# Gate and up products of a macaron decoder layer with the weight tile stationary and the tokens streamed

## The chip, the cores and the metric

One core of a Trainium2 chip runs one program that computes a whole decoder layer. The metric is device time in microseconds: 2391.34 us is the median of three runs (2390.54 to 2392.04). The profile is of one further execution, which took 2391.58 us; its span from the first to the last instruction is 2389.9 us.

## The reference, cut to what matters

```python
def swiglu(h, w_gate, w_up, w_down):
    return (jax.nn.silu(h @ w_gate) * (h @ w_up)) @ w_down

def rmsnorm(x, g):
    y = x * lax.rsqrt(jnp.mean(x * x, axis=-1, keepdims=True) + EPS)
    return y * g

x = x + 0.5 * swiglu(rmsnorm(x, ffn1_norm), ffn1_w_gate, ffn1_w_up, ffn1_w_down)   # half-step 1
h = rmsnorm(x, mix_norm)
mem_n = rmsnorm(mem, mem_norm)
x = x + mixer(h, mem_n, w_in, ..., w_kv_mem, w_branch, w_out)
x = x + 0.5 * swiglu(rmsnorm(x, ffn2_norm), ffn2_w_gate, ffn2_w_up, ffn2_w_down)   # half-step 2
return rmsnorm(x, final_norm)
```

x and mem are 256 tokens of 2048 features, float32. Gate and up weights are 2048 x 5632, the down weights 5632 x 2048. The mixer merges a gated linear attention, a spatial gating and an attention over the memory through 2048 x 12304 input weights, three branch weights of 1024 x 2048 and an output weight of 2048 x 2048.

## The kernel before, in words

All large products run in a rounded float32 format in which TensorE takes one pass per matmul. To keep float32 accuracy every operand is split in two: a rounded high part and the rounded remainder, low. A product is then three matmuls, high by high, high by low, low by high, summed in one PSUM accumulator (`products`, L123 to L125). Activations are kept transposed, as [features, tokens], in a `Split`: tiles of eight feature groups by 256 tokens, high and low. Weights come from HBM in 1 MB tiles `raw` of four feature groups by 512 columns (`load`, L112). `split` makes the parts of half such a tile, two feature groups, in one step: ScalarE casts it to `wh` (L119), VectorE subtracts to get `wl` (L120). `raw`, `wh` and `wl` have three buffers each. A half of a raw tile is called a half step below.

`gemm` runs one column chunk: 512 output features, all 256 tokens as two blocks b of 128, over all feature groups. In every matmul the 128 x 128 piece of the activations is the loaded operand and 512 weight columns stream past it, so the result is [128 tokens, 512 features] in one accumulator for each block.

`ffn` is a half-step of the layer (the reference's swiglu). Its 5632 hidden features are 11 chunks, done as a part of 6 and a part of 5; each part is followed by the four column chunks of the down product over its own features. For each chunk: the gate gemm; Silu with the row's norm factor `rs` (L319, tokens lie on partitions, so the factor is a per-partition scalar); the up gemm; a multiply by factor and Silu result (L323); and `tsplit` for each block, which transposes the four 128 x 128 pieces on TensorE (L166, into a `trp` bank) and splits them into high (L174) and low (L175) of `hT`, the loaded operand of the down product.

PSUM has eight banks, in three pools: four for accumulators `acc`, two for transposes `trp`, two for small products `sml`. The start of the program brings in the memory in four pieces, transposes and scales them (`norm_piece`, L190 and L191) and runs the four chunks of the memory's key and value product. The mixer lies between the half-steps; small generators are advanced one step per half step (`tick`) so that the branches' small work falls between the matmuls of the projections.

No order is written out by hand: the instructions of each engine are put in order ahead of time, by a scheduler that simulates the program with times of its own and hands out free buffers as they come up. So the number of buffers in a pool also sets the order of an engine's list. On the chip each engine then runs its list strictly in that order.

Of the kernel before, what the change touches and what calls it, by code (L numbers as in the profile page):

```python
# [8 lines left out]
F32 = mybir.dt.float32  # L9
# [3 lines left out]
AF = mybir.ActivationFunctionType  # L13
ALU = mybir.AluOpType
AX = mybir.AxisListType
PSUM = bass.MemoryType.PSUM

P = 128
S = 256
NB = S // P  # L20
D = 2048
KT = D // P
DFF = 5632
CW = 512
# [11 lines left out]
class Split:  # L36
# [11 lines left out]
    def l(self, kt, b):  # L48
        return self.lo[kt // 8][:, kt % 8, b * P : (b + 1) * P]

    def four(self, kt, b):
        i, j = kt // 8, kt % 8
        return (
            self.hi[i][:, j : j + 4, b * P : (b + 1) * P],
            self.lo[i][:, j : j + 4, b * P : (b + 1) * P],
        )
# [3 lines left out]
def layer(ctx: ExitStack, tc: tile.TileContext, a: dict, out: bass.AP):  # L60
    nc = tc.nc
    cp = ctx.enter_context(tc.tile_pool(name="cp", bufs=1))
# [1 line left out]
    wp = ctx.enter_context(tc.tile_pool(name="wp", bufs=3))  # L64
    tp = ctx.enter_context(tc.tile_pool(name="tp", bufs=5))
    sp = ctx.enter_context(tc.tile_pool(name="sp", bufs=4))
    pacc = ctx.enter_context(tc.tile_pool(name="pacc", bufs=4, space=PSUM))
    ptr = ctx.enter_context(tc.tile_pool(name="ptr", bufs=2, space=PSUM))
    psm = ctx.enter_context(tc.tile_pool(name="psm", bufs=2, space=PSUM))

    def slot(shape, dtype=F32):
        return big.tile(shape, dtype, name="m8", tag="m8")

    def tmp():
        return tp.tile([P, CW], F32, name="tmp", tag="tmp")

    def acc():
        return pacc.tile([P, CW], F32, name="acc", tag="acc")

    def trp():  # L80
        return ptr.tile([P, CW], F32, name="trp", tag="trp")

    def sml():
        return psm.tile([P, CW], F32, name="sml", tag="sml")

    x0 = a["x"][0]
    mem0 = a["mem"][0]
# [4 lines left out]
    def tick(n=1):  # L92
        for _ in range(n):
            while queue:
                try:
                    next(queue[0])
                    break
                except StopIteration:
                    queue.pop(0)
# [6 lines left out]
    def load(w, row, col, parts=1):  # L106

        raw = wp.tile([P, 4, CW], F32, name="raw", tag="raw")
        n = 4 // parts
        for i in range(0, 4, n):  # L110
            r = row + i * P
            nc.sync.dma_start(  # L112
                raw[:, i : i + n, :],
                w[r : r + n * P, col : col + CW].rearrange("(j p) n -> p j n", p=P),
            )
        return raw
# [7 lines left out]
        nc.tensor.matmul(acc, lhsT=lhs.h(kt, b), rhs=wl, start=False, stop=False)  # L124
        nc.tensor.matmul(acc, lhsT=lhs.l(kt, b), rhs=wh, start=False, stop=last)  # L125

    def gemm(lhs, n_tiles, w, row0, col0, accs, ticks=0, raws=(), tail=0):


        raws = list(raws)  # L130
        held = []
        for g0 in range(0, n_tiles, 4):
            raw = raws.pop(0) if raws else load(w, row0 + g0 * P, col0)
            late = g0 >= n_tiles - 4 * tail
            if late:
                both = [slot([P, 4, CW], F32R) for _ in range(2)]
                held.append((g0, *both))
            for h0 in (0, 2):
                if late:
                    wh, wl = (t[:, h0 : h0 + 2, :] for t in both)  # L140
                else:
                    wh = wp.tile([P, 2, CW], F32R, name="wh", tag="wh")
                    wl = wp.tile([P, 2, CW], F32R, name="wl", tag="wl")
                split(raw[:, h0 : h0 + 2, :], wh, wl)
                if late:
                    continue
                for b in range(NB):
                    for j in range(2):
                        kt = g0 + h0 + j
                        products(  # L150
                            lhs, kt, b, wh[:, j, :], wl[:, j, :], accs[b],
                            kt == 0, kt == n_tiles - 1,
                        )
                tick(ticks)
        for b in range(NB):
            for g0, wh, wl in held:
                for j in range(4):
                    kt = g0 + j
                    products(
                        lhs, kt, b, wh[:, j, :], wl[:, j, :], accs[b], kt == 0, kt == n_tiles - 1  # L160
                    )
# [9 lines left out]
    def tsplit(src, dst, kt, b):  # L171
        ps = transpose4(src).rearrange("p (j t) -> p j t", t=P)
        hi, lo = dst.four(kt, b)
        nc.scalar.copy(hi, ps)  # L174
        nc.vector.tensor_tensor(lo, ps, hi.bitcast(F32), op=ALU.subtract)  # L175
# [34 lines left out]
    def stats(name):  # L210
        return (
            cp.tile([P, NB, NCH], F32, name=f"ss_{name}"),
            cp.tile([P, NB], F32, name=f"rs_{name}"),
        )


    ident = cp.tile([P, P], F32, name="ident")
# [14 lines left out]


    ss_m, rs_m = stats("m")
    mem_s = [slot([P, NB, 2 * CW]) for _ in range(2)]
    memT = Split(slot, KT)
# [4 lines left out]
    first = []  # L241
# [12 lines left out]
    xT = Split(slot, KT)  # L254
# [33 lines left out]
    for c in range(4):  # L288
        accs = [acc() for _ in range(NB)]
# [5 lines left out]
        for b in range(NB):  # L295
            r = rs_m[:, b : b + 1]
            if c < 2:
                t = tmp()
# [8 lines left out]


    def ffn(xT, rs, wg, wu, wd, after, begin=lambda: None, final=False):
        done = 0  # L310
        for part, n_ch in enumerate((6, 5)):
            hT = Split(slot, 4 * n_ch)
            for c in range(n_ch):
                col = (done + c) * CW
                pg = [acc() for _ in range(NB)]
                gemm(xT, KT, wg, 0, col, pg, ticks=1)
                sil = [tmp() for _ in range(NB)]
                for b in range(NB):
                    nc.scalar.activation(sil[b], pg[b], AF.Silu, scale=rs[:, b : b + 1])  # L319
                pu = [acc() for _ in range(NB)]  # L320
                gemm(xT, KT, wu, 0, col, pu, ticks=1)
                for b in range(NB):
                    nc.vector.scalar_tensor_tensor(  # L323
                        out=sil[b], in0=pu[b], scalar=rs[:, b : b + 1], in1=sil[b],
                        op0=ALU.mult, op1=ALU.mult,
                    )
                    tsplit(sil[b], hT, 4 * c, b)
            if part == 1:
                begin()
            for n in range(NCH):  # L330
                pd = [acc() for _ in range(NB)]
                ends = final and part == 1 and n == NCH - 1
                gemm(
                    hT, 4 * n_ch, wd, done * CW, n * CW, pd, ticks=1, tail=2 if ends else 0
                )
                for b in range(NB):
                    xs = x_s[b][:, n * CW : (n + 1) * CW]
                    nc.vector.scalar_tensor_tensor(  # L338
                        out=xs, in0=pd[b], scalar=0.5, in1=xs, op0=ALU.mult, op1=ALU.add
                    )  # L340
                    if part == 1:
                        after(xs, b, n)
            done += n_ch
# [385 lines left out]
    for i in (1, 2, 0):  # L729
        for n in range(NCH):  # L730
            pg = [acc() for _ in range(NB)]
# [89 lines left out]
```

## Time and profile before

| | |
|---|---|
| median of three runs | 2391.34 us |
| profiled execution, span | 2391.58 us, 2389.9 us |
| TensorE matmuls busy | 2372.0 us (99%) |
| weight loads busy | 1961.7 us (82%) |
| VectorE, ScalarE busy | 1270.1 us (53%), 1071.5 us (45%) |
| HBM read | 445.84 MB, 188 GB/s |

Busy times count an engine's own instructions. A matmul's end is modelled and reaches past the start of the next one, so a busy TensorE says that work was queued, not how fast it went; for that one counts starts in a stretch. Matmuls of `acc` are 128 x 512 and those of `trp` 128 x 128; PE stands for TensorE's matmuls, PEld for its weight loads, DVE for VectorE, ACT for ScalarE, SP for the engine that issues the DMAs.

### The profile page before, as it was taken

To read this page: it belongs to the slowest core of one execution; us is meant where nothing else is said; L and a number is where in the kernel's file an instruction comes from. 1 tells how busy PE (TensorE), PEld (TensorE's weight loads), DVE (VectorE), ACT (ScalarE), POOL (GpSimd) and SP (SyncE) were. 2 spreads that over 40 slices of the span, in tenths; PEclk is the share of its full clock that TensorE was granted. 3 is DMA by queue.
4 is the path that set the end of the run, shared out by engine and by line. 5 is a ranking of instruction groups with operands and counts; after the bars stand their busy time and mean duration, and the time that the engine had idled before them with its cause. 6 is when DMAs were issued, how large, how long until landed. Compare 5 with 4: busy or idle time off the path is not lost.

```text
span 2389.9 us, 26431 instructions
## 1 busy us (share of the span) xinstructions
PE 2372.0 (99%) x10746; PEld 1961.7 (82%) x10746; DVE 1270.1 (53%) x1330; ACT 1071.5 (45%) x1265; POOL 59.5 (2%) x57
## 2 busy tenths in 40 slices
PE   8999999999999999999999999999999999999998
PEld 6888888888888888888788888888888888888886
DVE  5644545445445556556765555555454454454454
ACT  6544444344444444435444444445444433444443
POOL 0000000000000001001300000000000000000000
PEclk9999999999999999999999999999999999999999
DMA  7555555555555665454546555655555555555554
GB/s 257 190 188 187 190 194 191 193 193 187 188 194 193 196 210 191 148 169 159 176 159 211 194 194 194 203 185 191 186 189 191 193 189 193 194 184 193 194 191 144
DMA packets 224211, 451.76 MB, mean 189 GB/s; under 512 B 7268, under 2 KB 7336, under 8 KB 223448
## 3 DMA queue, kind: packets, MB, share of 16 engines
q1 hardware_dynamic: 222344, 442.56, 55.8%
q0 software_dynamic: 1744, 7.51, 0.9%
q8 instruction: 84, 1.38, 0.2%
q14 instruction: 39, 0.32, 0.0%
HBM read 445.84 MB, written 4.19 MB: 188 GB/s over the span
## 4 chain that ended last, share of the span: by engine, by line
PE 97%; DVE 1%; issue 1%; ACT 1%; DMA 0%; ACTq 0%; POOLq 0%; POOL 0%; SPq 0%; DVEq 0%
PE acc L124 31%; PE acc L123 31%; PE acc L125 31%; PE trp L166 2%; PE sml L641 0%; DVE wl L120 0%; PE sml L546 0%; PE sml L574 0%; PE sml L449 0%; DMA m<-in_mem_dram 0%; ACT m L658 0%; ACT tmp L180 0%; ACT wh L119 0%; PE sml L695 0%; PE sml L508 0%
## 5 line engine op out<-in xcount | busy, mean ns | idle before, releaser
L120 DVE TENSOR_TENSOR wl<-raw,wh 128x1024 fp32r<-128x1024 f32 x828 | 1029.4, 1244 | 1025.4 <-ACT wh L119 1024.8
L119 ACT CAST wh<-raw 128x1024 fp32r<-128x1024 f32 x828 | 871.5, 1053 | 1162.4 <-PE acc L125 1143.0
L124 PE MATMUL acc<-wl,m 128*128 128x512 f32 x3312 | 1294.7, 391 | 1.8 <-DVE wl L120 1.7
L125 PE MATMUL acc<-wh,m 128*128 128x512 f32 x3312 | 1290.6, 390 | 0.1
L123 PE MATMUL acc<-wh,m 128*128 128x512 f32 x3312 | 1184.2, 392 | 1.8 <-ACT wh L119 0.9
L124 PEld LDWEIGHTS acc<-wl,m 128*128 128x128 f32 x3312 | 622.6, 188 | 132.2 <-DVE wl L120 3.2
L123 PEld LDWEIGHTS acc<-wh,m 128*128 128x128 f32 x3312 | 622.2, 188 | 131.7 <-ACT m L190 2.2
L125 PEld LDWEIGHTS acc<-wh,m 128*128 128x128 f32 x3312 | 622.1, 188 | 127.5 <-DVE m L191 0.5
L190 ACT ACTIVATE m<-trp,gT 128x128 fp32r<-128x128 f32 x128 | 43.0, 364 | 23.7 <-PE trp L166 14.3
L174 ACT CAST m<-trp 128x512 fp32r<-128x512 f32 x64 | 34.9, 588 | 40.9 <-PE trp L166 40.9
L175 DVE TENSOR_TENSOR m<-trp,m 128x512 fp32r<-128x512 f32 x64 | 41.8, 687 | 21.2 <-ACT m L174 20.9
L191 DVE SCALAR_TENSOR_TENSOR m<-trp,gT,m 128x128 fp32r<-128x128 f32 x128 | 41.3, 347 | 13.4 <-ACT m L190 12.2
L166 PEld LDWEIGHTS trp<-ident,tmp 128*128 128x128 f32 x288 | 34.6, 140 | 6.7
L166 PE MATMUL trp<-ident,tmp 128*128 128x128 f32 x288 | 40.0, 272 | 0.0
L319 ACT ACTIVATE tmp<-acc,rs 128x512 f32<-128x512 f32 x44 | 30.1, 690 | 19.5 <-PE acc L125 19.5
L180 ACT ACTIVATE tmp<-m 128x512 f32<-128x512 f32 x40 | 24.8, 623 | 15.4 <-DVE m L338 11.8
L323 DVE SCALAR_TENSOR_TENSOR tmp<-acc,rs,tmp 128x512 f32<-128x512 f32 x44 | 30.9, 744 | 0.0
L338 DVE SCALAR_TENSOR_TENSOR m<-acc,m 128x512 f32<-128x512 f32 x32 | 20.9, 684 | 9.7 <-PE acc L125 9.4
L203 POOL TENSOR_TENSOR rs<-rs,mhalf 128x1 f32<-128x1 f32 x8 | 4.3, 552 | 868.5 <-DVE rs L200 868.5
L166 PE MATMUL trp<-ident,m 128*128 128x128 f32 x160 | 22.8, 280 | 2.8 <-DMA m<-in_mem_dram 2.8
L166 PEld LDWEIGHTS trp<-ident,m 128*128 128x128 f32 x160 | 19.6, 144 | 6.6 <-DMA m<-in_mem_dram 2.9
L661 POOL TENSOR_TENSOR m<-m,m 128x1024 f32<-128x1024 f32 x7 | 20.9, 2991 | 115.3 <-ACT m L658 87.8
(136 smaller groups left out, 389.1 us busy)
## 6 DMA issues: line engine op xcount, KB each, us to landing
raw<-in_w_in_dram SPq DMA_DIRECT2D x96, 1024.0 KB, 5.0
raw<-in_ffn_w_gate_dram SPq DMA_DIRECT2D x88, 1024.0 KB, 5.1
raw<-in_ffn_w_up_dram SPq DMA_DIRECT2D x88, 1024.0 KB, 5.1
raw<-in_ffn_w_down_dram SPq DMA_DIRECT2D x88, 1024.0 KB, 5.1
raw<-in_w_branch_dram SPq DMA_DIRECT2D x24, 1024.0 KB, 5.1
raw<-in_w_out_dram SPq DMA_DIRECT2D x16, 1024.0 KB, 5.1
raw<-in_w_kv_mem_dram SPq DMA_DIRECT2D x14, 1024.0 KB, 5.1
m<-in_mem_dram SPq DMA_DIRECT2D x4, 512.0 KB, 8.3
```

The costliest lines, as they stand in the source:

```text
L119: nc.scalar.copy(wh, raw)
L120: nc.vector.tensor_tensor(wl, raw, wh.bitcast(F32), op=ALU.subtract)
L123: nc.tensor.matmul(acc, lhsT=lhs.h(kt, b), rhs=wh, start=first, stop=False)
L124: nc.tensor.matmul(acc, lhsT=lhs.h(kt, b), rhs=wl, start=False, stop=False)
L125: nc.tensor.matmul(acc, lhsT=lhs.l(kt, b), rhs=wh, start=False, stop=last)
L166: nc.tensor.transpose(out=ps[:, j * P : (j + 1) * P], in_=src[:, j * P : (j + 1) * P], identity=ident)
L174: nc.scalar.copy(hi, ps)
L175: nc.vector.tensor_tensor(lo, ps, hi.bitcast(F32), op=ALU.subtract)
L190: nc.scalar.activation(dst.h(kt, b), pj, AF.Copy, scale=g)
L191: nc.vector.scalar_tensor_tensor(out=dst.l(kt, b), in0=pj, scalar=g, in1=dst.h(kt, b).bitcast(F32), op0=ALU.mult, op1=ALU.subtract,)
L319: nc.scalar.activation(sil[b], pg[b], AF.Silu, scale=rs[:, b : b + 1])
L323: nc.vector.scalar_tensor_tensor(out=sil[b], in0=pu[b], scalar=rs[:, b : b + 1], in1=sil[b], op0=ALU.mult, op1=ALU.mult,)
```

## The change

In the gate and up gemms the 128 x 128 piece of the weights becomes the loaded operand, and the activations' 256 tokens stream past it (`turned_products`). The result is [128 features, 256 tokens], four accumulators `acct` for a chunk of 512 features, each half a bank of data in a bank of its own. The result is already laid out as the down product needs it, so `tsplit` is not called there any more; `hT` is filled by a copy and a subtraction from SBUF. Tokens now lie along the free dimension, so the norm factor can no longer be a per-partition scalar: `token_factor` transposes it once per half-step into a row that all partitions hold, and VectorE multiplies by that row, before Silu (from PSUM) and after it. The three PSUM pools become one of eight banks for all uses. The down product and the mixer's gemms keep their form.

```diff
-    pacc = ctx.enter_context(tc.tile_pool(name="pacc", bufs=4, space=PSUM))
-    ptr = ctx.enter_context(tc.tile_pool(name="ptr", bufs=2, space=PSUM))
-    psm = ctx.enter_context(tc.tile_pool(name="psm", bufs=2, space=PSUM))
+    ps8 = ctx.enter_context(tc.tile_pool(name="ps8", bufs=8, space=PSUM))
...
+    def acct():
+        return ps8.tile([P, S], F32, name="acct", tag="ps")
...
+    def turned_products(rhs, kt0, wh, wl, accs, first, last):
+        for f in range(4):
+            fs = slice(f * P, (f + 1) * P)
+            for j in range(2):
+                hi, lo = rhs.both(kt0 + j)
+                w = wh[:, j, fs]
+                nc.tensor.matmul(accs[f], lhsT=w, rhs=hi, start=first and j == 0, stop=False)
+                nc.tensor.matmul(accs[f], lhsT=w, rhs=lo, start=False, stop=False)
+                nc.tensor.matmul(
+                    accs[f], lhsT=wl[:, j, fs], rhs=hi, start=False, stop=last and j == 1
+                )
...
+    def token_factor(rs, name):
+        ps = trp()
+        for b in range(NB):
+            nc.tensor.transpose(
+                out=ps[:, b * P : (b + 1) * P], in_=rs[:, b : b + 1].to_broadcast([P, P]),
+                identity=ident,
+            )
+        row = cp.tile([P, S], F32, name=name)
+        nc.vector.tensor_copy(row, ps[:, :S])
+        return row
...
-                pg = [acc() for _ in range(NB)]
-                gemm(xT, KT, wg, 0, col, pg, ticks=1)
-                sil = [tmp() for _ in range(NB)]
-                for b in range(NB):
-                    nc.scalar.activation(sil[b], pg[b], AF.Silu, scale=rs[:, b : b + 1])
-                pu = [acc() for _ in range(NB)]
-                gemm(xT, KT, wu, 0, col, pu, ticks=1)
-                for b in range(NB):
-                    nc.vector.scalar_tensor_tensor(
-                        out=sil[b], in0=pu[b], scalar=rs[:, b : b + 1], in1=sil[b],
-                        op0=ALU.mult, op1=ALU.mult,
-                    )
-                    tsplit(sil[b], hT, 4 * c, b)
+                pg = [acct() for _ in range(4)]
+                gemm(xT, KT, wg, 0, col, pg, ticks=1, turned=True)
+                if row is None:
+                    row = token_factor(rs, f"row{final:d}")
+                sil = [tmp() for _ in range(2)]
+                for i in range(2):
+                    for f in range(2):
+                        nc.vector.tensor_tensor(
+                            sil[i][:, f * S : (f + 1) * S], pg[2 * i + f], row, op=ALU.mult
+                        )
+                    nc.scalar.activation(sil[i], sil[i], AF.Silu)
+                    nc.vector.tensor_tensor(pairs(sil[i]), pairs(sil[i]), along(row), op=ALU.mult)
+                pu = [acct() for _ in range(4)]
+                gemm(xT, KT, wu, 0, col, pu, ticks=1, turned=True)
+                for i in range(2):
+                    for f in range(2):
+                        h = sil[i][:, f * S : (f + 1) * S]
+                        nc.vector.tensor_tensor(h, pu[2 * i + f], h, op=ALU.mult)
+                    hi, lo = hT.two(4 * c + 2 * i)
+                    nc.scalar.copy(hi, pairs(sil[i]))
+                    nc.vector.tensor_tensor(lo, pairs(sil[i]), hi.bitcast(F32), op=ALU.subtract)
```

TensorE's list at the program's first instructions, before (`gm` are the memory's norm gains, `m8_89` and `m8_90` the first and second half of the memory's features, `m8_91` and `m8_93` the high and low parts of its transposed form):

```order
L230 MATMUL trp_97<-ident_79,gm_95 128x16
L166 MATMUL trp_101<-ident_79,m8_89 128x128 x4
L166 MATMUL trp_114<-ident_79,m8_89 128x128 x4
L123 MATMUL acc_227<-wh_229,m8_91 128x512
L123 MATMUL acc_228<-wh_229,m8_91 128x512
L124 MATMUL acc_227<-wl_230,m8_91 128x512
L125 MATMUL acc_227<-wh_229,m8_93 128x512
```

And the same place of the changed kernel (`m8_83` and `m8_84` are the two halves of the memory, `m8_85` the high part):

```order
L275 MATMUL trp_91<-ident_73,gm_89 128x16
L193 MATMUL trp_95<-ident_73,m8_83 128x128 x4
L193 MATMUL trp_108<-ident_73,m8_83 128x128 x4
L193 MATMUL trp_125<-ident_73,m8_83 128x128 x4
L193 MATMUL trp_138<-ident_73,m8_83 128x128 x4
L193 MATMUL trp_155<-ident_73,m8_84 128x128 x4
L193 MATMUL trp_168<-ident_73,m8_84 128x128 x4
L193 MATMUL trp_184<-ident_73,m8_84 128x128 x4
L193 MATMUL trp_197<-ident_73,m8_84 128x128 x4
L131 MATMUL acc_221<-wh_223,m8_85 128x512
L132 MATMUL acc_221<-wl_224,m8_85 128x512
```

Before, eight transposes of the first memory piece stand ahead of the first product, and the other 24 further down, between products. In the changed list all 32 stand ahead of it, those of the second half too.

TensorE's list in half-step 1 at the end of one chunk's up product and the start of the next chunk's gate product, before (`acc_1623` and `acc_1624` are the next gate's accumulators, `tmp_1465` and `tmp_1466` the finished chunk):

```order
L124 MATMUL acc_1624<-wl_1644,m8_220 128x512
L125 MATMUL acc_1624<-wh_1643,m8_222 128x512
L166 MATMUL trp_1608<-ident_79,tmp_1465 128x128 x4
L166 MATMUL trp_1616<-ident_79,tmp_1466 128x128 x4
L123 MATMUL acc_1624<-wh_1643,m8_220 128x512
L124 MATMUL acc_1624<-wl_1644,m8_220 128x512
L125 MATMUL acc_1624<-wh_1643,m8_222 128x512
```

The same engine at such a place of the changed kernel (`acct_2993` belongs to the up product that ends, `acct_3236` and `acct_3237` to the next gate product; `m8_214` to `m8_217` hold the activations):

```order
L144 MATMUL acct_2993<-m8_217,wh_3198 128x256
L145 MATMUL acct_2993<-m8_215,wl_3199 128x256
L143 MATMUL acct_3236<-m8_214,wh_3242 128x256
L144 MATMUL acct_3236<-m8_216,wh_3242 128x256
L145 MATMUL acct_3236<-m8_214,wl_3243 128x256
L143 MATMUL acct_3236<-m8_214,wh_3242 128x256
L144 MATMUL acct_3236<-m8_216,wh_3242 128x256
L145 MATMUL acct_3236<-m8_214,wl_3243 128x256
L143 MATMUL acct_3237<-m8_214,wh_3242 128x256
L144 MATMUL acct_3237<-m8_216,wh_3242 128x256
```

The eight transposes are gone, one product follows on the other; each matmul writes 256 columns and there are twice as many.

VectorE's list over one chunk of half-step 1, before (the gate product ends within the first row, the up product before the second):

```order
L120 TENSOR_TENSOR wl<-raw,wh 128x1024 x14
L323 SCALAR_TENSOR_TENSOR tmp<-acc,rs_219,tmp 128x512 x2
L120 TENSOR_TENSOR wl<-raw,wh 128x1024 x2
L175 TENSOR_TENSOR m_988<-trp,m_985 128x4x128 x2
L120 TENSOR_TENSOR wl<-raw,wh 128x1024 x14
```

And of the changed kernel (`row_1262` is the token row, L367 and L371 the multiplies by it before and after Silu, L377 the multiply of up by the Silu result, L380 the low part of `hT`):

```order
L367 TENSOR_TENSOR tmp<-acct,row_1262 128x256
L128 TENSOR_TENSOR wl<-raw,wh 128x1024
L367 TENSOR_TENSOR tmp<-acct,row_1262 128x256 x3
L128 TENSOR_TENSOR wl<-raw,wh 128x1024
L371 TENSOR_TENSOR tmp<-tmp,row_1262 128x512 x2
L128 TENSOR_TENSOR wl<-raw,wh 128x1024 x6
L377 TENSOR_TENSOR tmp<-acct,tmp 128x256
L128 TENSOR_TENSOR wl<-raw,wh 128x1024
L377 TENSOR_TENSOR tmp<-acct,tmp 128x256 x3
L128 TENSOR_TENSOR wl<-raw,wh 128x1024
L380 TENSOR_TENSOR m_984<-tmp,m_981 128x512 x2
```

At the end of the gate product, where VectorE had nothing but splits, six multiplies now stand among three splits; at the end of the up product four multiplies and two subtractions take the place of two multiplies and two subtractions.

## Rows read from the trace of the kernel before

**Rows 1.** The page: busy time of each engine; the chain's shares by engine.

```profile
PE 2372.0 (99%) x10746; PEld 1961.7 (82%) x10746; DVE 1270.1 (53%) x1330; ACT 1071.5 (45%) x1265; POOL 59.5 (2%) x57
...
PE 97%; DVE 1%; issue 1%; ACT 1%; DMA 0%; ACTq 0%; POOLq 0%; POOL 0%; SPq 0%; DVEq 0%
```

**Rows 2.** Windows: down products; one chunk. Columns: busy (instructions) by engine, clock, DMA, GB/s.

```profile
420.00:520.00 100.00, 100.00 (x443) 82.80 (x442) 48.50 (x43) 39.04 (x37) 0.00 (x0) 1.00 0.59 192
...
689.36:733.77 44.41, 44.41 (x203) 36.86 (x202) 22.21 (x20) 19.22 (x21) 0.00 (x0) 1.00 0.57 189
```

**Rows 3.** Timeline of TensorE around a chunk's transposes: start us, us, engine, line.

```profile
732.98 1.03 PE L166 MATMUL trp<-ident,tmp 128*128 128x128 f32 x8
733.77 0.48 PE L123 MATMUL acc<-wh,m 128*128 128x512 f32 x1
734.09 0.40 PE L124 MATMUL acc<-wl,m 128*128 128x512 f32 x1
```

**Rows 4.** Timeline of VectorE and ScalarE in a gate product, idle time before in brackets.

```profile
713.18 1.22 DVE L120 TENSOR_TENSOR wl<-raw,wh 128x1024 fp32r<-128x1024 f32 x1 [1.49 <-ACT wh L119]
...
714.82 1.05 ACT L119 CAST wh<-raw 128x1024 fp32r<-128x1024 f32 x1 [1.67 <-PE acc L125]
```

**Rows 5.** Timeline of TensorE: low-rank projection (L449) between wide products; the following load.

```profile
768.54 0.28 PE L449 MATMUL sml<-m,gh 128*16 128x256 f32 x1
768.65 0.28 PE L449 MATMUL sml<-m,gl 128*16 128x256 f32 x1
768.77 0.39 PE L449 MATMUL sml<-m,gh 128*16 128x256 f32 x2
769.00 0.39 PE L124 MATMUL acc<-wl,m 128*128 128x512 f32 x1
769.23 0.39 PE L125 MATMUL acc<-wh,m 128*128 128x512 f32 x1
769.46 0.40 PE L123 MATMUL acc<-wh,m 128*128 128x512 f32 x1
...
768.89 0.19 PEld L124 LDWEIGHTS acc<-wl,m 128*128 128x128 f32 x1
```

**Rows 6.** Timeline of TensorE: scores of the linear attention (L641).

```profile
1126.66 1.27 PE L641 MATMUL sml<-m 128*128 128x128 f32 x10
1127.69 0.48 PE L124 MATMUL acc<-wl,m 128*128 128x512 f32 x1
```

**Rows 7.** Groups by line and form: count, busy us, mean ns, idle before.

```profile
L641 PEld LDWEIGHTS sml<-m 128*128 128x128 f32 x128 | 18.1, 190 | 2.0
...
L323 DVE SCALAR_TENSOR_TENSOR tmp<-acc,rs,tmp 128x512 f32<-128x512 f32 x44 | 30.9, 744 | 0.0
...
L175 DVE TENSOR_TENSOR m<-trp,m 128x512 fp32r<-128x512 f32 x64 | 41.8, 687 | 21.2 <-ACT m L174 20.9
...
L748 DVE TENSOR_TENSOR m<-m,tmp 128x512 f32<-128x512 f32 x16 | 10.3, 685 | 0.0
...
L512 DVE SCALAR_TENSOR_TENSOR tmp<-sml,gT,m 128x256 f32<-128x256 f32 x8 | 3.9, 483 | 3.3 <-PE sml L508 3.3
```

**Rows 8.** Timeline of the start, SyncE and TensorE.

```profile
7.07 0.38 SPq L244 DMA_DIRECT2D m<-in_mem_dram  x1
...
5.65 1.97 PE L166 MATMUL trp<-ident,m 128*128 128x128 f32 x8 [2.82 <-DMA m<-in_mem_dram]
8.20 1.22 PE L123 MATMUL acc<-wh,m 128*128 128x512 f32 x2 [0.58 <-ACT wh L119]
...
12.62 0.63 PE L123 MATMUL acc<-wh,m 128*128 128x512 f32 x1
13.04 0.63 PE L124 MATMUL acc<-wl,m 128*128 128x512 f32 x1
```

**Rows 9.** DMA issues from 7 to 8.6 us: count, size, median us to landing.

```profile
m<-in_mem_dram SPq DMA_DIRECT2D x2, 512.0 KB, 9.5
```

**Rows 10.** Window of the start, TensorE's matmuls into `acc` alone.

```profile
8.00:41.40 33.40, 30.73 (x109) 1.00 0.80 294
```

More of the change, by code (lines that the diff above doesn't have):

```diff
@@ L49, in l, with both, two @@
         return self.lo[kt // 8][:, kt % 8, b * P : (b + 1) * P]
+    def both(self, kt):
+        return self.hi[kt // 8][:, kt % 8, :], self.lo[kt // 8][:, kt % 8, :]
+    def two(self, kt):
+        i, j = kt // 8, kt % 8
+        return self.hi[i][:, j : j + 2, :], self.lo[i][:, j : j + 2, :]
     def four(self, kt, b):
@@ L77, in acc @@
     def acc():
-        return pacc.tile([P, CW], F32, name="acc", tag="acc")
+        return ps8.tile([P, CW], F32, name="acc", tag="ps")
+    def acct():
+        return ps8.tile([P, S], F32, name="acct", tag="ps")
     def trp():
-        return ptr.tile([P, CW], F32, name="trp", tag="trp")
+        return ps8.tile([P, CW], F32, name="trp", tag="ps")
     def sml():
-        return psm.tile([P, CW], F32, name="sml", tag="sml")
+        return ps8.tile([P, CW], F32, name="sml", tag="ps")
     x0 = a["x"][0]
@@ L125, in products, with gemm @@
         nc.tensor.matmul(acc, lhsT=lhs.l(kt, b), rhs=wh, start=False, stop=last)
-    def gemm(lhs, n_tiles, w, row0, col0, accs, ticks=0, raws=(), tail=0):
+    def turned_products(rhs, kt0, wh, wl, accs, first, last):
[9 more added lines that the diff above has]
+                )
+    def gemm(lhs, n_tiles, w, row0, col0, accs, ticks=0, raws=(), tail=0, turned=False):
         raws = list(raws)
@@ L145, in gemm @@
                 if late:
+                    continue
+                if turned:
+                    kt = g0 + h0
+                    turned_products(lhs, kt, wh, wl, accs, kt == 0, kt == n_tiles - 2)
+                    tick(ticks)
                     continue
@@ L214, in stats, with pairs, along @@
         )
+    def token_factor(rs, name):
[8 more added lines that the diff above has]
+        return row
+    def pairs(ap):
+        return ap.rearrange("p (f t) -> p f t", t=S)
+    def along(row):
+        return row.unsqueeze(1).to_broadcast([P, 2, S])
     ident = cp.tile([P, P], F32, name="ident")
@@ L309, in ffn @@
     def ffn(xT, rs, wg, wu, wd, after, begin=lambda: None, final=False):
-        done = 0
+        done, row = 0, None
         for part, n_ch in enumerate((6, 5)):
```

## The prediction

> **What bounds the kernel now.** I read the page's busy line first, then the chain that ended last, then windows of single stretches, then the timeline of the places that the change touches. TensorE is busy for 99% of the span and the chain lies on it for 97% [rows 1]. A busy share alone could hide waits, so the pace counts: in the hundred microseconds from 420 to 520, which hold down products only, 443 matmuls touch the window. Two are cut by its edges, so about 441 fit, or 226.7 ns for one 512-column matmul with its own 128x128 weight load, at the upper clock level of 2.4 GHz (granted clock 1.00) [rows 2]. The time of this kernel is therefore the length of TensorE's list, and a change is worth what it does to that list.
>
> One column chunk of 512 features in a half-step takes 44.41 us [rows 2]. Its gate and up products are 2 x 16 x 2 x 3 = 192 matmuls: 192 x 226.67 ns = 43.52 us. The other 0.89 us is the eight transposes that turn the chunk's result: they start at 732.98, the next product starts at 733.77, and the one behind it only 314 ns later instead of 227 [rows 3]. Nothing else in the chunk stops TensorE. VectorE and ScalarE follow it: of each half step of 2.72 us (12 matmuls, one split of 1024 weight columns) ScalarE waits 1.67 us for TensorE and VectorE 1.49 us for ScalarE [rows 4].
>
> **The change, part by part.**
>
> *Transposes that go.* 22 chunks (11 in each half-step) lose eight each: 22 x 0.89 = 19.7 us off the path. Nothing takes their place on TensorE except four transposes in all for the token row: about 0.5 us at the 0.11 us of rows 3.
>
> *Matmuls that change shape.* 22 x 192 = 4224 matmuls of 512 columns become 8448 of 256 columns. The multiplied work is the same; the weight loads double. If 256 columns take half of 512, 113.3 ns, this costs nothing; every nanosecond above that costs 8.4 us. So this one number decides the sign. The trace has 256-column matmuls in the same number format, those of the low-rank projection: four that start at 768.54 end with the next product's start at 769.00, 115 ns each [rows 5]. The last of them had the 128x128 load of the following product beside it (issued at 768.89), so a full load goes under 256 columns in about 113 ns. Against that stands that the 512-column products behind the four start 230 and 230 ns apart (rounded as the rows have it), a little slower than the settled 226.7, and that these are short bursts with 16-column loads between them. The other near row is the score products of the linear attention: ten pairs of a 128x128 load and a 128-column two-pass matmul run from 1126.66 to 1127.69 [rows 6], 103 ns each with both ends counted. Loads at that rate would fit under 113. Bounds: 0 from the proportional reading; below it I see no reason, since the 512-column pace is already the proportional one; above it 6.7 ns, if the 13.3 ns by which 226.7 exceeds 512/2.4 = 213.3 is paid by every matmul whatever its width (106.7 + 13.3 = 120.0; 56 us in all). I take 0, since 115 for the burst is nearer to 113.3 than to 120.
>
> The Trainium skill ("Perfetto Trace Analysis", section Identifying the Most-Contended Engine) says the reverse of the busy line: TensorE's headroom is to be judged by the weight loads' busy share. Here that share is 82% already [rows 1], and 4224 more loads of 188 ns would take it past the span. The 128 score loads last 190 ns each, 24.3 us in sum, and cover only 18.1 us [rows 7]: loads overlap each other, so the sum of their lengths is no bound. By the rule the change would cost hundreds of microseconds, by the row nothing; it is kept as a rival below.
>
> *Work that moves to VectorE and ScalarE.* A chunk gains on VectorE eight 256-column multiplies (0.48 each by the nearest row that reads the accumulators) and four 512-column ones (0.69), 6.6 us, and loses two of 0.74 and two of 0.69, 2.9 us [rows 7]; with 22.2 us busy in 44.4 [rows 2] it goes to about 26. ScalarE keeps two Silu and two copies. The cover is the three-deep split buffers: a split ends 2.3 us after its buffers come free and is needed after 5.4 [rows 4]. The order puts one multiply, a split, three multiplies, a split, and the last two multiplies behind the gate product. The split queued in the middle waits on ScalarE for two Silu (1.4 us), which wait for the last multiplies, 0.5 us behind the product's end: 0.5 + 1.4 + 1.05 + 1.23 = 4.2 us of the 5.4. The stall is zero, with a margin of a microsecond at each of the 44 product ends; if it ran out by 0.2 us each it would cost 9 us.
>
> *PSUM in one pool.* Gate and up take four banks each, all eight, but the gate's come free within 2 us of its end and are needed 21 us later. The mixer shares the eight too. Before, no wait for a bank stands among TensorE's; I take 0, bounds -2 (more room) and +5.
>
> *The start.* This is the part the diff does not show. With two transpose banks only eight transposes of the memory went ahead of the first product, the others lay between products. With eight banks all 32 go first, in TensorE's own order, and they need the last memory piece. Its last two pieces are issued from 7.07 on, one behind the other [rows 8], and land a median 9.5 us after issue [rows 9]; I take 18 us for the later one. Eight cold transposes took 1.97 us [rows 8]. So the first product starts at 18 + 2 = about 20 us instead of 8.20. Then TensorE is cold: before, the matmuls after 12.62 start 420 ns apart (two decimals), which is 512/1.2 = 427 ns at the lower clock level, 1.2 GHz [rows 8], and some thirteen products had passed when they quickened. I allow as many again: 13 x 427 ns end at 25.6, then one per 226.7 ns makes 70 more by 41.4, 83 in all. Before, 109 matmul records lie between 8.00 and 41.40 [rows 10]. The deficit is 26 x 0.2267 = 5.9 us. Bounds: 3 us, if the many early transposes already raise the clock; 8 us, if the splits behind the 16 norm pieces come late as well.
>
> **Sum.** -19.7 + 0.5 + 0 + 0 + 0 + 5.9 = -13.3 us. The profiled execution took 2391.6 us, of which 2389.9 are the span; the median of the runs shown is 2391.3, the same within 0.02%. So 2378 us.
>
> **Rivals.**
>
> *The narrow products never settle at half.* Mechanism: a 256-column matmul in a long run keeps the 117 ns that the middle ones of the burst show (768.65 to 768.77 and on to 769.00, two starts merged) [rows 5], because a load is in flight nearly all the time. 8448 x 3.7 = +31 us: 2409, slower than before. For it: the burst's mean is 115 and the wide products behind it are slow too. Against it: part of the burst is at 113, and the score pairs ran faster. It turns the result into a loss from 13.3 / 8.448 = 1.6 ns on, that is 114.9 ns per matmul. At 120 ns (the fixed-excess bound) it would be 2434.
>
> *Half way.* The pace is 114 to 115.5, and the start and the excess eat the transposes' gain: 2387 to 2396, no change that can be told.
>
> *Loads bind.* Each load holds the path for its 188 ns: 8448 x (188 - 113.3) = +631 us, about 3010. The overlap in rows 7 speaks against it.
>
> The page named above would give this last time. A further page, "TensorE: Matmul & The Clock Gate" of the Trainium skill (section LDWEIGHTS), puts a load at its columns over 1.2 GHz, an estimate of 107 ns for 128 columns: by that it just hides under 113 ns, and no run here shows it for a long run.
>
> *The start is cheaper or dearer, all else as forecast:* 2375 to 2381; it moves the number, not the sign.
>
> **How the numbers follow.** What a measurement of this kernel can tell from no change is 0.2%, 4.8 us. Forecast with its neighbours (2370 to 2386): 0.53. Half way: 0.13. Narrow products at 117 to 120: 0.30. Loads bind or worse: 0.04. That the change does nothing at all is excluded by TensorE's order, where the transposes are gone. Faster 0.53, same 0.13, slower 0.34. Both signs hold weight, so the range reaches from 2371 (start at its low bound, mixer a little better) to 2414 (117 ns plus some of the mixer's bound); the likeliest case's own range is 2371 to 2384.
>
> **What would show it.** In the changed trace: a chunk of 43.5 us with 384 matmuls starting 113.3 ns apart says that the pace is half; 45 says 117. No transposes inside the half-steps' chunks. The first 512-column product at about 20 us, not 8. ScalarE's and VectorE's splits still ending their waits on TensorE and not the reverse; TensorE waiting for a split at a product's end would prove the cover too thin. The prediction is wrong if the pace passes 114.9 ns, or if TensorE waits for accumulators.

## The result and the profile after

The changed kernel takes 2448.49 us (median of 4 runs, 2447.72 to 2448.66), the kernel before on the same chip 2391.28 us: ratio 1.0238, 95% interval 1.0226 to 1.0251. It is 57.2 us slower; 13 us faster was forecast, and the range ended at 2414.

The page of the changed kernel: the engines, to be held against [rows 1], and one of its new groups (count, busy us, mean ns, idle before):

```profile
PE 2412.2 (99%) x14798; PEld 2167.2 (89%) x14798; DVE 1324.3 (54%) x1508; ACT 1064.2 (43%) x1266; POOL 60.7 (2%) x57
...
L145 PE MATMUL acct<-m,wl 128*128 128x256 f32 x2816 | 795.9, 283 | 0.0
```

TensorE is still 99% busy, and the new group (L143 and L144 have as many and read the same) shows no idle time. From the busy line alone nothing looks lost. The pace tells. Windows of the changed kernel, gate and up products first, then down products:

```profile
150.00:250.00 100.00, 100.00 (x836) 100.00 (x835) 52.32 (x59) 40.85 (x43) 0.00 (x0) 1.00 0.56 181
...
420.00:520.00 100.00, 100.00 (x443) 82.84 (x442) 48.87 (x43) 38.86 (x37) 0.00 (x0) 1.00 0.59 192
```

The down products have the 443 matmuls of [rows 2]. In the gate and up products 836 touch the window; less some two and a half that its edges cut, 833.5 fit, so one starts every 120.0 ns at granted clock 1.00. A matmul is shown as 283 ns long and a load as 192, so both rows are full at 100.00 at any pace from 192 down; only the count separates 113 from 120.

The same from VectorE's side (its timeline, with idle time before in brackets; L377 multiplies the up's accumulators, L128 are the splits; a gate product ended at 183):

```profile
160.04 0.42 DVE L377 TENSOR_TENSOR tmp<-acct,tmp 128x256 f32<-128x256 f32 x1 [1.42 <-PE acct L145]
...
189.13 1.23 DVE L128 TENSOR_TENSOR wl<-raw,wh 128x1024 fp32r<-128x1024 f32 x1 [0.51 <-ACT wh L127]
192.00 1.23 DVE L128 TENSOR_TENSOR wl<-raw,wh 128x1024 fp32r<-128x1024 f32 x1 [1.64 <-ACT wh L127]
...
206.12 0.42 DVE L377 TENSOR_TENSOR tmp<-acct,tmp 128x256 f32<-128x256 f32 x1 [1.42 <-PE acct L145]
```

From one up product's end to the next, 160.04 to 206.12, a chunk takes 46.08 us, where [rows 2] have 44.41 with the transposes in it: 384 x 120.0 ns and no stop. The splits start 2.87 us apart, 24 matmuls, and wait for ScalarE; even the one behind the six multiplies and two Silu of the gate's end (189.13) was held 0.51 us by ScalarE and not by VectorE's own work.

The waits of TensorE (line, what it waited for, us in all, times, longest) are new, however; before had 2.8 us for the memory [rows 8], 2.5 for the identity matrix and 3.4 for splits and norm pieces, and nothing else:

```profile
PE trp L193 <- DMA m<-in_mem_dram: 10.1, 3, 4.9
PE trp L193 <- DVE m L801: 5.9, 4, 1.5
...
PE trp L193 <- ACT tmp L581: 1.9, 2, 1.6
PE acc L132 <- DVE wl L128: 1.2, 1, 1.2
PE trp L193 <- DVE m L391: 1.1, 4, 0.3
PE trp L193 <- DVE m L815: 1.1, 4, 0.3
PE trp L193 <- ACT tmp L344: 0.4, 1, 0.4
```

Only one is for a split. The others are transposes (L193) of results that VectorE or ScalarE has just made, outside the chunks. The worst of them on TensorE's timeline, in the mixer:

```profile
1488.10 0.39 PE L133 MATMUL acc<-wh,m 128*128 128x512 f32 x1
1489.98 1.26 PE L193 MATMUL trp<-ident,m 128*128 128x128 f32 x8 [1.48 <-DVE m L801]
1490.99 0.47 PE L131 MATMUL acc<-wh,m 128*128 128x512 f32 x1
```

The transposes stand directly behind the last matmul of the product whose result they turn. TensorE starts nothing for 1.88 us where 0.23 is usual: 1.65 us lost, 1.48 of them shown as idle. Before, work of the next product stood between (L748 is the line that L801 has become):

```profile
1462.34 0.69 DVE L748 TENSOR_TENSOR m<-m,tmp 128x512 f32<-128x512 f32 x1
...
1466.28 0.62 PE L123 MATMUL acc<-wh,m 128*128 128x512 f32 x2
1466.73 1.03 PE L166 MATMUL trp<-ident,m 128*128 128x128 f32 x8
```

VectorE was done at 1463.03, 3.7 us before the transposes began, and TensorE had matmuls until then.

The start, to be held against [rows 8]:

```profile
10.09 1.97 PE L193 MATMUL trp<-ident,m 128*128 128x128 f32 x8 [2.46 <-DMA m<-in_mem_dram]
16.92 3.67 PE L193 MATMUL trp<-ident,m 128*128 128x128 f32 x16 [4.86 <-DMA m<-in_mem_dram]
20.25 0.78 PE L131 MATMUL acc<-wh,m 128*128 128x512 f32 x1
20.82 0.63 PE L132 MATMUL acc<-wl,m 128*128 128x512 f32 x1
...
22.53 0.51 PE L133 MATMUL acc<-wh,m 128*128 128x512 f32 x1
22.88 0.40 PE L131 MATMUL acc<-wh,m 128*128 128x512 f32 x1
```

The first product starts at 20.25 us, as foreseen: by the trace the last memory piece landed at 18.26. The lower clock level of the first matmuls is read from their spacing, here as in [rows 8] (20.82 to 22.53 are four steps of 427 ns, 512 columns at 1.2 GHz); the clock column of the windows reads 1.00 for this stretch in both kernels, [rows 10] too.

### The profile page after: what moved, and what is told of

It reads as the page before. It is cut to its first block, busy times and chain, and to the rows that moved or that the text cites. A ratio compares the mean times of both kernels' runs of the same rounds, so it can differ in the third digit from the quotient of the medians.

```text
span 2446.9 us, 34812 instructions
## 1 busy us (share of the span) xinstructions
PE 2412.2 (99%) x14798; PEld 2167.2 (89%) x14798; DVE 1324.3 (54%) x1508; ACT 1064.2 (43%) x1266; POOL 60.7 (2%) x57
## 3 DMA queue, kind: packets, MB, share of 16 engines
q8 instruction: 115, 1.88, 0.3%
## 4 chain that ended last, share of the span: by engine, by line
PE 96%; DVE 2%; ACT 1%; issue 1%; DMA 1%; SPq 0%; ACTq 0%; POOLq 0%; POOL 0%; DVEq 0%
PE acc L132 17%; PE acc L133 17%; PE acc L131 17%; PE acct L144 14%; PE acct L145 14%; PE acct L143 14%; PE trp L193 1%; DVE wl L128 1%; ACT wh L127 1%; PE sml L694 1%; DMA m<-in_mem_dram 0%; PE sml L599 0%; PE sml L627 0%; PE sml L502 0%; DMA raw<-in_w_kv_mem_dram 0%
## 5 line engine op out<-in xcount | busy, mean ns | idle before, releaser
L128 DVE TENSOR_TENSOR wl<-raw,wh 128x1024 fp32r<-128x1024 f32 x828 | 1027.1, 1241 | 978.7 <-ACT wh L127 978.5
L143 PE MATMUL acct<-m,wh 128*128 128x256 f32 x2816 | 797.0, 283 | 0.0
L144 PE MATMUL acct<-m,wh 128*128 128x256 f32 x2816 | 796.7, 283 | 0.0
L145 PE MATMUL acct<-m,wl 128*128 128x256 f32 x2816 | 795.9, 283 | 0.0
L132 PE MATMUL acc<-wl,m 128*128 128x512 f32 x1904 | 743.8, 391 | 1.3 <-DVE wl L128 1.2
L133 PE MATMUL acc<-wh,m 128*128 128x512 f32 x1904 | 742.7, 390 | 0.0
L131 PE MATMUL acc<-wh,m 128*128 128x512 f32 x1904 | 688.4, 393 | 0.0
L144 PEld LDWEIGHTS acct<-m,wh 128*128 128x128 f32 x2816 | 540.6, 192 | 0.1
L143 PEld LDWEIGHTS acct<-m,wh 128*128 128x128 f32 x2816 | 540.6, 192 | 0.1
L145 PEld LDWEIGHTS acct<-m,wl 128*128 128x128 f32 x2816 | 540.2, 192 | 0.0
L132 PEld LDWEIGHTS acc<-wl,m 128*128 128x128 f32 x1904 | 357.9, 188 | 75.4 <-DVE wl L128 2.4
L133 PEld LDWEIGHTS acc<-wh,m 128*128 128x128 f32 x1904 | 357.8, 188 | 74.1
L131 PEld LDWEIGHTS acc<-wh,m 128*128 128x128 f32 x1904 | 357.7, 188 | 73.3 <-issue 0.8
L377 DVE TENSOR_TENSOR tmp<-acct,tmp 128x256 f32<-128x256 f32 x88 | 33.8, 422 | 31.1 <-PE acct L145 31.1
L367 DVE TENSOR_TENSOR tmp<-acct,row 128x256 f32<-128x256 f32 x88 | 33.5, 421 | 28.4 <-PE acct L145 28.4
L193 PE MATMUL trp<-ident,m 128*128 128x128 f32 x160 | 27.5, 311 | 18.4 <-DMA m<-in_mem_dram 10.1
L193 PEld LDWEIGHTS trp<-ident,m 128*128 128x128 f32 x160 | 20.4, 157 | 27.5 <-DMA m<-in_mem_dram 11.0
L371 DVE TENSOR_TENSOR tmp<-tmp,row 128x512 f32<-128x512 f32 x44 | 28.3, 685 | 0.2 <-ACT tmp L370 0.2
```

Source lines behind the costliest of these rows:

```text
L128: nc.vector.tensor_tensor(wl, raw, wh.bitcast(F32), op=ALU.subtract)
L131: nc.tensor.matmul(acc, lhsT=lhs.h(kt, b), rhs=wh, start=first, stop=False)
L143: nc.tensor.matmul(accs[f], lhsT=w, rhs=hi, start=first and j == 0, stop=False)
L144: nc.tensor.matmul(accs[f], lhsT=w, rhs=lo, start=False, stop=False)
L145: nc.tensor.matmul(accs[f], lhsT=wl[:, j, fs], rhs=hi, start=False, stop=last and j == 1)
L193: nc.tensor.transpose(out=ps[:, j * P : (j + 1) * P], in_=src[:, j * P : (j + 1) * P], identity=ident)
```

## The experiments

Theory: a matmul with a 128-column load in this number format takes its columns at 2.4 GHz and 13.3 ns more, whatever its width, so cutting 512 into two of 256 adds 6.7 ns per narrow matmul. Rivals: the turned form itself is slow (weights loaded right after they are written, tokens streamed); the evacuation work starves TensorE; the single pool does it. Differences below are taken from 2391.28 us; the kernel before, run again beside the experiments, had medians of 2390.74 and, for the last two, 2391.23 us, and the ratios are to these, so half a microsecond of a difference means nothing.

**Narrow matmuls in the old form.** The kernel before, with its three pools, its orientation and its transposes; only the gate and up matmuls are cut in two, except the first of each accumulator.

```diff
-                        products(
+                        (narrow_products if narrow else products)(
...
+        for i in range(2):
+            cs = slice(i * S, (i + 1) * S)
+            for k, (x, w) in enumerate(pairs):
+                nc.tensor.matmul(
+                    acc[:, cs], lhsT=x, rhs=w[:, cs], start=False,
+                    stop=last and i == 1 and k == len(pairs) - 1,
+                )
```

> The kernel before with one thing changed: in the gate and up gemms every 512-column matmul is cut into two of 256 columns, with the same loaded activations, the same accumulators, transposes and pools (the first matmul of each accumulator stays whole). Of the 192 matmuls of a chunk 188 become 376. Theory 1, every matmul pays about 13.3 ns on top of its columns (256 columns: 120.0 ns): 22 x (376 x 0.120 - 188 x 0.22667) = +55 us, 2446 us, and a chunk of 46.9 us. Rival, the pace of 120 ns comes from the turned form (weights as the loaded operand, just written by ScalarE and VectorE): 2391 us, a chunk stays at 44.4 us.

Measured 2446.14 us, ratio 1.0231 (1.0216 to 1.0247): +54.9 us. Its window of gate and up products:

```profile
150.00:250.00 100.00, 100.00 (x829) 99.60 (x829) 48.05 (x44) 40.56 (x43) 0.00 (x0) 1.00 0.55 180
```

Cut are 4224 - 88 matmuls, into 8272: x 6.67 ns = 55.2 us. The count of 829 is that of 120.0 ns with the chunks' transposes and a few whole matmuls in the window; from one up product's multiplies to the next (154.75 to 201.64 in its trace) a chunk takes 46.89 us, the 46.9 of theory 1. Halving the width, which doubles the loads with it, costs the whole amount with neither the turned form nor its evacuation nor the one pool. The rivals on form and evacuation are not needed.

**The change with the pools of before.** Gate accumulators in the four banks of `acc`, the up's in the two of `trp` and the two of `sml`.

```diff
-    def acct():
-        return ps8.tile([P, S], F32, name="acct", tag="ps")
+    def acct(i, up):
+        pool, tag = (pacc, "acc") if not up else (ptr, "trp") if i < 2 else (psm, "sml")
+        return pool.tile([P, S], F32, name="acct", tag=tag)
```

> The changed kernel with the three PSUM pools of before (4 + 2 + 2 banks; gate accumulators in the four, up accumulators in the other four). Theory, the single pool costs the 15 to 20 us beyond the narrow matmuls, by the order it gives TensorE's list at the start and in the mixer: first product at about 8 us, no wait of 1.9 us ahead of the transposes of the mixer, total 2391.3 - 19.7 + 56.3 + 0.5 = 2428 us. Rival, these microseconds come from the turned products themselves (other engines late, other transfers): about 2448 us as the changed kernel.

Measured 2428.87 us, ratio 1.0159 (1.0144 to 1.0174). Waits of TensorE and the window:

```profile
PE trp L196 <- DMA m<-in_mem_dram: 2.9, 1, 2.9
...
PE acc L135 <- DVE wl L131: 1.8, 3, 0.9
```

```profile
150.00:250.00 100.00, 100.00 (x836) 100.00 (x835) 54.79 (x64) 41.34 (x45) 0.00 (x0) 1.00 0.56 185
```

The pace is the same 836, the waits are those of the kernel before, and the first product starts at 8.33 us. So the turned products with their transposes saved cost 2428.87 - 2391.28 = 37.6 us, which is 56.3 - 19.7 + 0.5 = 37.1 by the terms; the pool costs the other 2448.49 - 2428.87 = 19.6 us.

**One pool, and nothing else.** The kernel before with its three pools made one of eight banks.

```diff
-    pacc = ctx.enter_context(tc.tile_pool(name="pacc", bufs=4, space=PSUM))
-    ptr = ctx.enter_context(tc.tile_pool(name="ptr", bufs=2, space=PSUM))
-    psm = ctx.enter_context(tc.tile_pool(name="psm", bufs=2, space=PSUM))
+    ps8 = ctx.enter_context(tc.tile_pool(name="ps8", bufs=8, space=PSUM))
```

> The kernel before with one thing changed: one PSUM pool of eight banks for all. Theory, as for the kernel with three pools: the start costs 5.4 us and the mixer 11.8 us as in the changed kernel, and the transposes of each chunk, which now stand directly behind the up product in TensorE's list, wait about 0.5 us each for VectorE: 22 x 0.5 = 11 us more; 2391.3 + 5.4 + 11.8 + 11 = 2420 us. Rival, the pool is innocent: 2391 us.

Measured 2427.48 us, ratio 1.0154 (1.0137 to 1.0171): +36.2 us, more than expected. Waits of TensorE, then its timeline at the end of a chunk in half-step 1:

```profile
PE trp L164 <- DMA m<-in_mem_dram: 10.1, 3, 4.9
PE trp L164 <- DVE tmp L321: 7.6, 22, 0.3
PE trp L164 <- DVE m L746: 5.9, 4, 1.5
```

```profile
158.03 0.39 PE L123 MATMUL acc<-wh,m 128*128 128x512 f32 x1
158.77 1.31 PE L164 MATMUL trp<-ident,tmp 128*128 128x128 f32 x8 [0.35 <-DVE tmp L321]
159.84 0.47 PE L121 MATMUL acc<-wh,m 128*128 128x512 f32 x1
```

The waits of the mixer are there as in the changed kernel (the largest item is 5.9 us in four waits). On top, all 22 chunks wait at their transposes, which the changed kernel no longer has: 158.77 - 158.03 = 0.74 us where 0.23 is usual, and 1.07 us from the transposes' start to the next product, against 0.79 in [rows 3]: 0.79 us a chunk, 17 us in all. I had expected two thirds of that. So the pool works through the order: transposes stand directly behind the product that feeds them, and TensorE waits out the evacuation. That the scheduler does so because a bank is free for them earlier is argued from how it hands out buffers, not shown.

**Pace by width.** Behind the end of the kernel before, eleven runs of 96 matmuls (nine are shown) on TensorE alone, all operands long since in SBUF, loaded and streamed columns varied. The time of the program says nothing here.

```diff
+    for k in range(NP):
+        nc.tensor.matmul(pw[:128, :256], lhsT=src[:, k % 8, :128], rhs=m[:, k % 4 * 256 : k % 4 * 256 + 256], start=k == 0, stop=k == NP - 1)
```

> The kernel before, and behind its end eleven runs of 96 matmuls in the rounded format, one after the other on TensorE alone: (loaded columns, streamed columns) 128/512, 128/384, 128/256, 128/192, 128/128, 64/256, 16/256, 64/128, 16/128, 128/320, 128/256. Read: ns from start to start within a run. Theory 1, a fixed excess of 13.3 ns for each matmul at 2.4 GHz: 226.7, 173.3, 120.0, 93.3, 66.7, 120.0, 120.0, 66.7, 66.7, 146.7, 120.0. Theory 2, the pace is proportional to the streamed columns (0.4427 ns each) but a load of 128 columns binds at 120 ns, shorter loads less: 226.7, 170.0, 120.0, 120.0, 120.0, 113.3, 113.3, 60, 56.7, 141.7, 120.0.

TensorE's timeline; the pace of a run is the distance of its start from the next run's, over 96 (the shape has the loaded columns ahead, 128*64 is 64, and the streamed behind, 128x256):

```profile
2401.43 21.92 PE L804 MATMUL sml<-m,m 128*128 128x512 f32 x96
2423.19 16.83 PE L806 MATMUL sml<-m,m 128*128 128x384 f32 x96
2439.85 11.67 PE L808 MATMUL sml<-m,m 128*128 128x256 f32 x96
2451.36 10.86 PE L810 MATMUL sml<-m,m 128*128 128x192 f32 x96
2462.06 10.86 PE L812 MATMUL sml<-m,m 128*128 128x128 f32 x96
2472.75 11.06 PE L814 MATMUL sml<-m,m 128*64 128x256 f32 x96
2483.65 11.04 PE L816 MATMUL sml<-m,m 128*16 128x256 f32 x96
2494.53 5.92 PE L818 MATMUL sml<-m,m 128*64 128x128 f32 x96
2500.28 5.92 PE L820 MATMUL sml<-m,m 128*16 128x128 f32 x96
```

With 128 loaded columns: 226.7 ns at 512, 173.5 at 384, 119.9 at 256; each is the columns over 2.4 GHz and 13.2 to 13.5 ns more. The run at 320 columns, not shown, has 147.2 ns, 13.9 more. At 192 and 128 streamed columns it is 111.5 and 111.4: none of these runs with loads of 128 columns is faster than that. With 64 or 16 loaded columns 256 streamed ones take 113.5 and 113.3 ns, a little under the 115 of [rows 5], whose loads had 16 columns. Neither theory holds whole: the first fits 128-column loads from 256 streamed columns up, the second has the shorter loads right and a floor by the load, but at 111 ns and not at 120. The Trainium skill ("TensorE: Matmul & The Clock Gate", section Back-to-back issue gap) gives columns over 2.4 GHz plus 2.5 ns for the gap of an isolated matmul, not for a stream of loads and matmuls, an estimate of 109.2 ns for 256; no run here goes as low with 256 columns in this format.

**High and low tokens side by side.** The changed form with three pools, but one 512-column matmul of [high, low] for each `wh` piece and one of 256 columns for `wl`: 5632 matmuls and loads instead of 8448. The two halves of an accumulator are added on the way out.

```diff
-                nc.tensor.matmul(accs[f], lhsT=w, rhs=hi, start=first and j == 0, stop=False)
-                nc.tensor.matmul(accs[f], lhsT=w, rhs=lo, start=False, stop=False)
+                if not end:
+                    nc.tensor.matmul(accs[f], lhsT=wh[:, j, fs], rhs=both, start=first and j == 0, stop=False)
+                nc.tensor.matmul(accs[f][:, :S], lhsT=wl[:, j, fs], rhs=hi, start=False, stop=False)
...
+                        nc.scalar.copy(sf, g[:, S:])
+                        nc.vector.tensor_tensor(sf, g[:, :S], sf, op=ALU.add)
```

> The changed form with three pools as before (2428.9 us), but high and low tokens lie side by side and stream as one 512-column matmul past each wh piece; wl keeps its 256 columns against the high tokens. 5632 matmuls with their loads instead of 8448; the two halves of an accumulator are added on VectorE after a copy by ScalarE. Theory (every matmul behind a 128-column load pays a fixed 13.3 ns): 2816 matmuls fewer x 13.3 ns = 37.5 us less, 2391 us, the same as before, with a chunk of 128 x 226.7 + 128 x 120.0 = 44.4 us. Rival (the cover of the splits was just thick enough; four more copies and four more additions at each of the 44 product ends let TensorE wait 0.5 to 1 us for a split): 2413 to 2435 us, with waits of TensorE on wl or wh at product ends. Rival (weights that are loaded right after being written cost something of their own): no more than half of the 37.5 comes back, 2410 us or more.

Measured 2398.83 us, ratio 1.0032 (1.0019 to 1.0044): 30.0 of the 37.5 us came back, 7.6 us stay. Waits of TensorE, then ScalarE's first copies behind two up products in a row:

```profile
PE trp L201 <- DMA m<-in_mem_dram: 2.7, 1, 2.7
...
PE acc L140 <- DVE wl L136: 1.8, 3, 0.9
```

```profile
153.17 0.37 ACT L389 COPY tmp<-acct 128x256 f32<-128x256 f32 x1
...
197.89 0.36 ACT L389 COPY tmp<-acct 128x256 f32<-128x256 f32 x1
```

No wait for a split is added, so the rival of the thin cover falls, and four fifths came back, so the one of freshly written weights falls too. A chunk takes 197.89 - 153.17 = 44.72 us, 0.35 more than 128 x 226.7 + 128 x 120.0 = 44.37; x 22 = 7.7 us, all that is left. A wide and a narrow matmul in turn take 349.4 ns together, 2.7 more than each in a run of its own kind. The fixed amount is thus good to a few ns here, not a law.

**Pace by load.** Ten more runs of 96 behind the kernel before, in the same manner (eight are shown).

```diff
+    for k in range(NP):
+        nc.tensor.matmul(pw[:64, :512], lhsT=src[:, k % 8, :64], rhs=m[:, k % 4 * 512 : k % 4 * 512 + 512], start=k == 0, stop=k == NP - 1)
```

> The kernel before with ten runs of 96 matmuls behind its end, TensorE alone, rounded format, loaded/streamed columns. Theory (a fixed amount per matmul that depends on the load's columns alone: 13.3 ns at 128, 6.7 ns at 64 or fewer, over streamed columns at 2.4 GHz; and a floor of about 111 ns that a 128-column load sets): 128/512 226.7, 64/512 and 16/512 220, 32/256 113.3, 32/128 60, 128/64 111, 64/64 about 56 (half the floor), 96/256 between 113.3 and 120. Rival (the smaller excess belongs to narrow streams): 64/512 and 16/512 stay at 226.7 and the low-rank rows are no special case of 16-column loads. The time of the whole program says nothing.

```profile
2423.03 22.24 PE L806 MATMUL sml<-m,m 128*64 128x512 f32 x96
2445.11 22.14 PE L808 MATMUL sml<-m,m 128*16 128x512 f32 x96
2467.08 11.30 PE L810 MATMUL sml<-m,m 128*96 128x256 f32 x96
2478.23 11.47 PE L812 MATMUL sml<-m,m 128*32 128x256 f32 x96
2489.53 11.68 PE L814 MATMUL sml<-m,m 128*128 128x256 f32 x96
2501.05 8.30 PE L816 MATMUL sml<-m,m 128*96 128x128 f32 x96
2509.19 5.92 PE L818 MATMUL sml<-m,m 128*32 128x128 f32 x96
2514.95 17.89 PE L820 MATMUL sml<-m,m 128*128 128x64 f32 x96
```

128/256 is 120.0 again. But 64/512 takes 230.0 and 16/512 228.9, not 220, and 32/256 takes 117.7, not 113.3. So the theory falls: the excess is not a function of the load's columns alone; smaller loads help a 256-column stream by 2 to 7 ns and a 512-column one not at all, as the rival had it for the wide streams. As expected were 96/256 (116.1, between) and 32/128 (60.0). With 96 loaded and 128 streamed columns it is 84.8 ns, which like the 111.4 of 128 loaded ones is some 0.87 to 0.88 ns for each loaded column. The last two runs, 128/64 and 64/64, tell nothing of the pace as a whole, since the clock changed (below).

What stays open is where the 13.3 ns come from. They are not in every matmul at every clock: at the lower level the wide matmuls of the start stand 427 ns apart, just 512/1.2. That a narrow matmul behind a 128-column load takes 120.0 ns, where two halves of a wide one would take 113.3, is shown four times: in the changed kernel, in the old form cut in two, and in both probes.

## Why the prediction was wrong

**The matmuls that change shape** are the step that failed. The term was put at 0, by the proportional reading of 113.3 ns, and measured 8448 x 6.7 ns = +56 us, the upper bound that the step itself had named (a fixed 13.3 ns for every matmul, 120.0). The choice between the ends went by the nearest row, and that row was near in the wrong respect: [rows 5] have the same format and the same 256 streamed columns but 16-column loads, and 113.3 ns is what such loads give in a long run as well. The prediction saw the 16-column loads and counted on the one 128-column load behind the burst; that load belonged to a wide product, which itself was slow by 3 ns. The score pairs of [rows 6] were misread: their ten matmuls make nine steps, from 1126.66 to 1127.66 (the last is 0.27 us long in the trace and ends the row's 1.27), 111 ns each, and the 103 came from counting the 0.03 us into the following product as a tenth. Read so, they are no faster than the 111.4 ns that 128-column loads hold in the probe; that still fits under 113.3 and says nothing of an excess at 256 columns. Both probes hold the row that was missing before, a run of narrow matmuls in this format each with its own 128-column load. The range then left out the step's own upper bound: with 56 us the sum is 2434, and the range ended at 2414.

**PSUM in one pool** was put at 0 with +5 as its upper bound; with the start apart it measured 19.6 - 5.2 = 14.4 us. The step looked for waits on banks, and there is none. What it missed is that the same sentence that explained the start (more free banks, transposes earlier in the order) holds at other transposes of the program too. The waits of L193 that are not for the memory sum to 10.4 us in 15 places, and each loses some 0.16 us more than is shown, as at 1488.10: 12.8 us. In the twelve where eight transposes waited for VectorE it is also some 0.22 us longer from them to the next product (1489.98 to 1490.99 against the 0.79 of [rows 3]), 2.6 us; together that is a microsecond more than was measured, which is left open.

**Transposes that go**, -19.7 us: right. None is left in the chunks, and the kernel with three pools comes within a microsecond of the sum with this term. **The start**, +5.9: 86 matmul records into `acc` lie between 8.00 and 41.40 against the 109 of [rows 10], 23 x 0.2267 = 5.2 us; the product began where foreseen, but six matmuls passed at the lower clock instead of thirteen. **Work on VectorE and ScalarE**, 0: right, one wait of 1.2 us for a split in the whole program; a multiply from the accumulators took 0.42 us where 0.48 was allowed. **Loads bind**: the loads' busy share went to 89% and the loads of a window fill it to 100.00, yet their length does not set the time; by their 192 ns 8448 of them would take 1622 us, and the gate and up products took 8448 x 120.0 ns = 1014.

The first rival had the right side and named its end, 2434 at 120 ns; the pool's 14.4 us make 2448 of that. Its own price, 117 ns and 2409 us, was too low, and its reason, a load in flight nearly all the time, no run shows. Two lesser sums of the prediction are off and change nothing: a pace of 114 ns gives 2384 and not 2387, and the low bounds of start and pool give 2373 and not 2371.

## What to carry to other kernels

Swapping the loaded and the streamed operand is no exchange of equals where it halves the streamed columns: price it per matmul with its own load, from a run that has the same format and load width. Here the fixed excess of the wide matmul, 13.3 ns, would have been the better forecast; in the probes it held behind 128-column loads from 256 to 512 streamed columns, and not at 192 and fewer. A pool of buffers that is shared or widened can change the order that a scheduler lays down; look in the new order for every consumer that now stands directly behind its producer, not only at the places that the edit touches. Transposes between products are cheap while other matmuls stand ahead of them: 0.89 us for eight, and nearly twice that (0.89 + 0.79) where they waited in the chunks of the kernel with one pool.

None of the variants beats the kernel before; the nearest, with the tokens paired, gives back in its narrow matmuls all that the missing transposes save (128 x 6.7 ns against 0.89 us a chunk).

## What was not expected of the hardware

In this format a 512-column stream behind 64- or 16-column loads is no faster than behind 128-column ones (230.0 and 228.9 against 226.7 ns), though 256- and 128-column streams are. And TensorE's clock fell while its row was full. Windows of the last probe, in its run of 64-column streams behind 128-column loads (the share ahead of the last two columns is the granted clock):

```profile
2515.00:2517.00 2.00, 2.00 (x21) 2.00 (x19) 0.00 (x0) 0.00 (x0) 0.00 (x0) 1.00 0.03 8
2520.00:2532.00 12.00, 12.00 (x58) 12.00 (x58) 0.00 (x0) 0.00 (x0) 0.00 (x0) 0.50 0.00 0
```

The run began at the upper level, 2.4 GHz; from 2520 on, and by the trace already from 2518, the granted clock was 0.50, 1.2 GHz, with matmuls and loads queued all the time, and the starts went from about 0.11 us apart (21 touch 2.00 us, some two of them begun before), the 111 ns expected, to 0.21 (58 touch 12.00). What made the clock fall no run shows.
